# A mixture-of-experts kernel: four of eight experts, not three, on the 64-slot f32 path

## The chip, the cores and the metric

The kernel runs on one core of a Trainium2 chip. The metric is device time in microseconds of one launch, the median of three runs. Five engines work beside each other and meet at semaphores: TensorE (PE, matrix products), VectorE (DVE), ScalarE (ACT), GpSimd (POOL) and SyncE (SP), which here issues nearly all loads from the chip's main memory (HBM) into on-chip memory. The loads run on 16 DMA engines.

## What is computed

A trunk of two layers over 256 latent tokens of 1024 numbers. Layer 0 is attention and a dense SwiGLU; layer 1 is a gated convolution and a mixture of eight experts, of which each token takes two. The change lies in the mixture of experts:

```python
def swiglu(h, w_gate, w_up, w_down):
    return (jax.nn.silu(h @ w_gate) * (h @ w_up)) @ w_down

def moe_swiglu(h, router_w, w_gate, w_up, w_down):
    logits = (h @ router_w).astype(jnp.float32)
    top_vals, top_idx = lax.top_k(logits, TOP_K)
    weights = jax.nn.softmax(top_vals, axis=-1)
    gates = jnp.sum(jax.nn.one_hot(top_idx, N_EXPERTS) * weights[..., None], axis=-2)
    out = gates[..., 0:1] * swiglu(h, w_gate[0], w_up[0], w_down[0])
    for e in range(1, N_EXPERTS):
        out = out + gates[..., e:e + 1] * swiglu(h, w_gate[e], w_up[e], w_down[e])
    return out
```

All is f32. An expert has gate and up matrices of 1024 x 3584 and a down matrix of 3584 x 1024: 44 MB in all, 352 MB for the eight.

## The kernel before

**Ranks and slots.** The 256 tokens make 512 picks, so a list has 64 tokens on average. The kernel sorts experts by the length of their lists (function `ranks`): expert 0 always has rank 1, so that its weights can be loaded before the sort is known, and the others follow, longest first. The first `NE - NL` ranks are *heavy* and have 128 slots, the last `NL` are *light* and have `CAP` = 64. A list longer than its slots sets a flag, and a second pass over all eight experts (`spill`) does the rest; it is left out when the flag is 0.

**Chunks.** Each expert's 3584 hidden columns are done in seven chunks of 512 (`NFC`). A chunk takes six tiles of 1 MB from HBM: gate and up for the first half of the 1024 inputs, the same for the second half, and two of the down matrix. The down product of a chunk is computed while the next chunk is on, after its gate and up products.

**A heavy chunk** has f32 weights which ACT (line 75) and DVE (line 76) split into two parts `hi` and `lo`, in halves of a tile (`parts`), twelve splits for a chunk. PE then makes three products in the faster `fp32r` form (`mac`, lines 305, 307, 309): 48 of 128 x 512 for gate and up, 24 for down. The parts lie in a pool of five pairs, so splits run at most about five halves ahead of PE. A raw tile is free again when it is split.

**A light chunk** takes the raw tiles as they are. `pair` (line 1371) makes one f32 product for each of two halves of PE's columns, 64 slots each: gate in one half and up in the other, or two halves of the down matrix's columns. A light chunk has 16 such matmuls for gate and up and 8 for down, and the profile records each as two. A raw tile is free when PE has used it.

```python
def pair(ps, lhsT, ws, first, last):
    for m, w in enumerate(ws):
        pe.matmul(ps[m * CAP:(m + 1) * CAP], lhsT, w, start=first, stop=last, tile_position=(0, m * CAP))
```

**The order of chunks** comes from a list, written out below. The first four chunks are heavy, the last four light, and the rest are merged evenly by `sorted`. With H for heavy and L for light, the order before is HHHHH L HH L HH L H L HH L ... HH L H LLLL (35 H, 21 L).

```python
heavy = [(r, c) for r in range(NE - NL) for c in range(NFC)]
light = [(r, c) for r in range(NE - NL, NE) for c in range(NFC)]
mixed = [((2 * n + 1) / len(v), m, rc) for m, v in enumerate((heavy[4:], light[:-4])) for n, rc in enumerate(v)]
chunks = heavy[:4] + [rc for *_, rc in sorted(mixed)] + light[-4:]
```

**Loads.** SP issues the tiles in the order of the chunks into a ring of 13 tiles (`spare`, `load`, line 68). A load waits until the tile that stood in its place is free, and those behind it wait with it. When a new expert is due, two chunks ahead, POOL gathers its tokens' rows (`fetch_rows`, line 1284) into a tile of the same ring; PE transposes them (`turn_rows`, line 1298) one chunk ahead, and with that the tile is free. When an expert is done, its rows go back to the tokens by a product with the one-hot matrix (`output`, `scatter`, line 1391).

Of the kernel before, what the change touches and what calls it, by code (L numbers as in the profile page):

```python
# [20 lines left out]
FC = 512  # L21
NFC = 3584 // FC
NG = 2816 // 256
NL = 3
CAP = 64
EPS = 1e-6
FLAT = [*range(20, 24), *range(28, 40), 44, 45]
# [7 lines left out]
def trunk(ctx, tc, i, out, dbg=None):  # L35
# [52 lines left out]
# [4 lines that stand above are left out]
# [3 lines left out]
    def weights(m, r, c, h):  # L95
        def ap():
            if r and r not in who:
                who[r] = nc.values_load(cur["who"][0:1, r:r + 1], engines=[mybir.EngineType.SP], min_val=0, max_val=NE - 1)
            return i[m][who[r] if r else 0, c, h]
        return ap  # L100

    whole += [False] * len(order)
    for n in range(len(chunks) + 1):
        if n < len(chunks):
            order += [weights(m, *chunks[n], h) for h in range(2) for m in ("moe_g", "moe_u")]
            whole += [chunks[n][0] >= NE - NL] * 4
        if n:
            order += [weights("moe_d", *chunks[n - 1], h) for h in range(2)]
            whole += [chunks[n - 1][0] >= NE - NL] * 2
    LEAD = 7  # L110
# [1094 lines left out]
    def ranks():  # L1205
# [19 lines left out]
        cur["who"] = idx  # L1225
        dve.tensor_scalar(cap, rank, NE - NL + 0.5, CAP - 128.0, op0=OP.is_gt, op1=OP.mult)
        dve.tensor_scalar(cap, cap, 128.0, None, op0=OP.add)
# [182 lines left out]
    for r, E in enumerate(experts):  # L1410
        E.r, E.light = r, r >= NE - NL
        E.ys, E.eh, E.el = [None, None], [None, None], [None, None]
# [287 lines left out]
```

## Time and profile before

| what | value |
|---|---|
| median of three runs | 1395.54 us (1393.89 to 1396.03) |
| the profiled execution: its time / its span | 1395.5 us / 1393.6 us |
| PE busy | 1353.8 us, 97% |
| DVE busy, ACT busy | 964.0 us (69%), 796.5 us (57%) |
| bytes read from HBM | 470.22 MB, of them 352 MB for the experts |
| chain that ended last | PE 85%, DMA 6%, DVE 4%, ACT 3% |

The span is the time from the first to the last instruction; what lies between it and the run's time is outside the program. Matmuls overlap each other in PE's pipeline, so a mean duration of one matmul is longer than the time from one to the next, and a PE that shows 97% need not be at its peak. The mixture of experts takes from about 495 us to the end.

### The profile page before, as it was taken

To read this page: it belongs to the slowest core of one execution; us is meant where nothing else is said; L and a number is where in the kernel's file an instruction comes from. 1 tells how busy PE (TensorE), PEld (TensorE's weight loads), DVE (VectorE), ACT (ScalarE), POOL (GpSimd) and SP (SyncE) were. 2 spreads that over 40 slices of the span, in tenths; PEclk is the share of its full clock that TensorE was granted. 3 is DMA by queue.
4 is the path that set the end of the run, shared out by engine and by line. 5 is a ranking of instruction groups with operands and counts; after the bars stand their busy time and mean duration, and the time that the engine had idled before them with its cause. 6 is when DMAs were issued, how large, how long until landed. Compare 5 with 4: busy or idle time off the path is not lost.

```text
span 1393.6 us, 19980 instructions
## 1 busy us (share of the span) xinstructions
PE 1353.8 (97%) x7496; PEld 990.2 (71%) x7496; DVE 964.0 (69%) x1257; ACT 796.5 (57%) x1070; POOL 10.8 (1%) x13
## 2 busy tenths in 40 slices
PE   6988999999999999999999999999999999999997
PEld 4766789999889977766666766667667666676742
DVE  4777768677677688866767767767577677676721
ACT  5566765444464377756656666656567566565610
POOL 0000000000000000000000000000000000000000
PEclk9999999999999999999999999999999999999999
DMA  9733778678657399797999999998999999999994
GB/s 374 281 121 117 277 270 334 242 284 311 251 237 266 147 380 358 274 420 320 420 420 421 420 380 420 409 400 365 419 413 422 415 374 386 408 421 417 416 421 166
DMA packets 67161, 473.70 MB, mean 340 GB/s; under 512 B 7472, under 2 KB 8112, under 8 KB 11120
## 3 DMA queue, kind: packets, MB, share of 16 engines
q1 hardware_dynamic: 66240, 469.46, 84.2%
q0 software_dynamic: 816, 2.88, 0.6%
q8 instruction: 61, 1.00, 0.3%
q14 instruction: 44, 0.36, 0.1%
HBM read 470.22 MB, written 2.10 MB: 339 GB/s over the span
## 4 chain that ended last, share of the span: by engine, by line
PE 85%; DMA 6%; DVE 4%; ACT 3%; issue 1%; SPq 0%; ACTq 0%; DVEq 0%
PE pm L1371 10%; PE pm L305 8%; PE pm L307 8%; PE pm L309 8%; PE acc L305 8%; PE acc L307 7%; PE acc L309 7%; PE acc L1371 5%; DMA raw<-in_moe_g_dram 5%; PE pm L961 4%; PE pm L963 4%; PE pm L962 4%; PE pm L1351 2%; DMA raw<-in_moe_d_dram 1%; PE pm L186 1%; DVE lo L76 1%
## 5 line engine op out<-in xcount | busy, mean ns | idle before, releaser
L76 DVE TENSOR_TENSOR lo<-raw,hi 128x1024 fp32r<-128x1024 f32 x522 | 628.6, 1222 | 157.1 <-ACT hi L75 133.1
L75 ACT ACTIVATE hi<-raw 128x1024 fp32r<-128x1024 f32 x522 | 545.6, 1060 | 256.5 <-PE pm L309 107.7
L305 PE MATMUL pm<-hi,eh 128*128 128x512 f32 x560 | 226.2, 404 | 0.4 <-ACT g L291 0.2
L307 PE MATMUL pm<-lo,eh 128*128 128x512 f32 x560 | 220.2, 393 | 2.2 <-DVE lo L76 2.0
L309 PE MATMUL pm<-hi,el 128*128 128x512 f32 x560 | 219.5, 392 | 0.0
L1371 PE MATMUL pm<-raw,hl 128*64 128x512 f32 x672 | 155.4, 599 | 0.0
L963 PE MATMUL pm<-th,lo 128*128 128x256 f32 x480 | 135.9, 283 | 0.0
L962 PE MATMUL pm<-tl,hi 128*128 128x256 f32 x480 | 135.7, 283 | 0.0
L961 PE MATMUL pm<-th,hi 128*128 128x256 f32 x480 | 135.6, 283 | 0.0
L305 PEld LDWEIGHTS pm<-hi,eh 128*128 128x128 f32 x560 | 105.8, 189 | 33.9 <-issue 8.1
L307 PEld LDWEIGHTS pm<-lo,eh 128*128 128x128 f32 x560 | 106.0, 189 | 24.5 <-DVE lo L76 4.6
L309 PEld LDWEIGHTS pm<-hi,el 128*128 128x128 f32 x560 | 105.7, 189 | 22.9
L1371 PEld LDWEIGHTS pm<-raw,hl 128*64 128x64 f32 x672 | 44.1, 136 | 80.5 <-issue 77.6
L961 PEld LDWEIGHTS pm<-th,hi 128*128 128x128 f32 x480 | 91.2, 190 | 0.8 <-issue 0.4
L962 PEld LDWEIGHTS pm<-tl,hi 128*128 128x128 f32 x480 | 91.0, 189 | 0.4
L963 PEld LDWEIGHTS pm<-th,lo 128*128 128x128 f32 x480 | 91.1, 190 | 0.0
L305 PE MATMUL acc<-hi,dh 128*128 128x512 f32 x280 | 88.7, 398 | 0.0
L307 PE MATMUL acc<-lo,dh 128*128 128x512 f32 x280 | 86.5, 390 | 0.0
L309 PE MATMUL acc<-hi,dl 128*128 128x512 f32 x280 | 86.3, 389 | 0.0
L1365 DVE TENSOR_TENSOR sg<-pm,sg 128x512 f32<-128x512 f32 (+1 forms) x56 | 38.5, 688 | 64.5 <-ACT sg L1364 64.2
L1371 PE MATMUL acc<-raw,dT 128*64 128x512 f32 x336 | 78.1, 600 | 0.0
L1364 ACT ACTIVATE sg<-pm 128x512 f32<-128x512 f32 (+1 forms) x56 | 32.7, 584 | 69.5 <-PE pm L1371 66.4
(331 smaller groups left out, 1568.0 us busy)
## 6 DMA issues: line engine op xcount, KB each, us to landing
raw<-in_moe_d_dram SPq DMA_DIRECT2D x112, 1024.0 KB, 12.8
raw<-in_moe_g_dram SPq DMA_DIRECT2D x111, 1024.0 KB, 12.9
raw<-in_moe_u_dram SPq DMA_DIRECT2D x111, 1024.0 KB, 12.8
raw<-in_ada_w_dram SPq DMA_DIRECT2D x48, 1024.0 KB, 6.2
raw<-in_conv_i_dram SPq DMA_DIRECT2D x12, 1024.0 KB, 7.0
raw<-in_ffn_g_dram SPq DMA_DIRECT2D x11, 1024.0 KB, 6.9
raw<-in_ffn_u_dram SPq DMA_DIRECT2D x11, 1024.0 KB, 4.8
raw<-in_ffn_d_dram SPq DMA_DIRECT2D x11, 1024.0 KB, 4.9
```

Source lines behind the costliest of these rows:

```text
L75: act.activation(hi, r, AF.Copy)
L76: dve.tensor_sub(lo, r, hi.bitcast(F32))
L305: pe.matmul(p, hh, wh[j], start=first, stop=False)
L307: pe.matmul(p, hh, wl[j], start=False, stop=False)
L309: pe.matmul(p, hl, wh[j], start=False, stop=last)
L961: pe.matmul(d, hi[:, c], th[:, k], start=(k == 0), stop=False)
L962: pe.matmul(d, hi[:, c], tl[:, k], start=False, stop=False)
L963: pe.matmul(d, lo[:, c], th[:, k], start=False, stop=(k == KD - 1))
L1351: pe.transpose(C.ps[:, k * w:(k + 1) * w], C.hd[:, k * 128:(k + 1) * 128], ident[0:w, 0:w])
L1364: act.activation(sg, C.g, AF.Silu)
L1365: dve.tensor_mul(sg, C.u, sg)
L1371: pe.matmul(ps[m * CAP:(m + 1) * CAP], lhsT, w, start=first, stop=last, tile_position=(0, m * CAP))
```

## The change

One constant: the four lowest ranks are light, not three.

```diff
 NFC = 3584 // FC
 NG = 2816 // 256
-NL = 3
+NL = 4
 CAP = 64
```

`NL` decides which ranks are heavy, which loads are taken whole (without a split), the slots of each rank, and by the list above the order of chunks. There are now 28 H and 28 L: HHHHH L H L H L ... H L LLLL, where H and L alternate from the fifth chunk on, and the last four are L as before.

On PE, the first place that differs is behind the down product of chunk 5, the first light one (`acc<-raw,dT`). `pm<-hi,eh` is a heavy gate or up product, `pm<-raw,hl` a light one, `cid,sg` the transposes of the chunk before. Before:

```order
L307 MATMUL pm<-lo,eh_5292 128x512
L309 MATMUL pm<-hi,el_5293 128x512
L1371 MATMUL acc<-raw,dT 64x512 x8
L305 MATMUL pm<-hi,eh_5270 128x512
L307 MATMUL pm<-lo,eh_5270 128x512
```

And now:

```order
L1371 MATMUL acc<-raw,dT 64x512 x8
L1371 MATMUL pm<-raw,hl 64x512 x6
L1351 MATMUL pm<-cid,sg 128x128 x4
L1371 MATMUL pm<-raw,hl 64x512 x10
L305 MATMUL acc<-hi,dh 128x512 x2
L307 MATMUL acc<-lo,dh 128x512 x2
L309 MATMUL acc<-hi,dl 128x512 x2
```

Chunk 7 was heavy, with 48 products for gate and up; it is light, with 16. The down product of chunk 6 follows it.

On SP, the same place in the queue of loads. A load that has an `ISA` row ahead of it takes its address from the expert number that SP reads from the sort, so it belongs to a rank above 1:

```order
 L68 DMA raw<-in_moe_d_dram 128x2048
-L68 DMA raw<-in_moe_g_dram 128x2048
-L68 DMA raw<-in_moe_u_dram 128x2048
-L68 DMA raw<-in_moe_g_dram 128x2048
-L68 DMA raw<-in_moe_u_dram 128x2048
-L68 DMA raw<-in_moe_d_dram 128x2048 x2
+L68 ISA
+L68 DMA raw<-in_moe_g_dram 128x2048
+L68 ISA
+L68 DMA raw<-in_moe_u_dram 128x2048
```

The tiles are as many as before (SP has 1005 rows in both), and gate, up and down follow each other as before. What moves is whose tiles they are: from here every second chunk's tiles are a light expert's.

## Rows read from the trace of the kernel before

**Rows 1.** The page: PE's share, then DMA share and GB/s in 40 slices.
```profile
PE 1353.8 (97%) x7496; PEld 990.2 (71%) x7496; DVE 964.0 (69%) x1257; ACT 796.5 (57%) x1070; POOL 10.8 (1%) x13
...
DMA  9733778678657399797999999998999999999994
GB/s 374 281 121 117 277 270 334 242 284 311 251 237 266 147 380 358 274 420 320 420 420 421 420 380 420 409 400 365 419 413 422 415 374 386 408 421 417 416 421 166
```

**Rows 2.** Stretches: busy time of each engine, granted clock, DMA share, GB/s.
```profile
579.00:1371.50 792.50, 786.71 (x3528) 513.47 (x3530) 541.49 (x534) 462.80 (x539) 8.27 (x6) 1.00 0.98 404
1371.50:1393.60 22.10, 13.49 (x64) 4.36 (x60) 3.92 (x6) 1.08 (x3) 0.00 (x0) 0.92 0.15 52
653.50:805.00 151.50, 149.38 (x672) 101.26 (x672) 108.59 (x104) 92.28 (x102) 1.76 (x1) 1.00 1.01 420
...
898.50:901.80 3.30, 3.30 (x9) 2.54 (x9) 3.27 (x5) 0.80 (x2) 0.00 (x0) 0.50 0.99 407
```

**Rows 3.** The chain that ended last, in order of time: start, us, what.
```profile
653.56 20.82 DMA raw<-in_moe_g_dram
...
1126.79 1.87 PE pm L1371 x8
...
1174.14 1.87 PE pm L1371 x8
...
1206.99 2.58 PE pm L1371 x12
...
1255.81 2.73 PE pm L1371 x12
...
1301.35 2.73 PE pm L1371 x12
...
1329.85 2.58 PE pm L1371 x12
...
1343.13 2.73 PE pm L1371 x12
...
1355.73 2.58 PE pm L1371 x12
...
1378.56 4.47 PE acc L1371 x20
1383.05 0.76 DVE raw L1529
```

**Rows 4.** Groups by line: count, busy and mean of one, idle before.
```profile
L76 DVE TENSOR_TENSOR lo<-raw,hi 128x1024 fp32r<-128x1024 f32 x522 | 628.6, 1222 | 157.1 <-ACT hi L75 133.1 <-issue 1.2
...
L305 PE MATMUL pm<-hi,eh 128*128 128x512 f32 x560 | 226.2, 404 | 0.4 <-ACT g L291 0.2
...
L1371 PE MATMUL pm<-raw,hl 128*64 128x512 f32 x672 | 155.4, 599 | 0.0
```

**Rows 5.** Timeline of SP's issues of loads: start, us.
```profile
564.76 2.61 SPq L68 DMA_DIRECT2D raw<-in_moe_d_dram  x2
578.98 0.33 SPq L68 DMA_DIRECT2D raw<-in_moe_g_dram  x1
...
624.55 0.33 SPq L68 DMA_DIRECT2D raw<-in_moe_u_dram  x1
643.41 0.91 SPq L68 DMA_DIRECT2D raw<-in_moe_d_dram  x2
644.56 0.33 SPq L68 DMA_DIRECT2D raw<-in_moe_g_dram  x1
```

**Rows 6.** What SP's queue waited for: us in total, times, longest.
```profile
SPq L68 <- PE pm L1371: 186.8, 36, 18.4
...
SPq L68 <- PE pm L1298: 58.3, 5, 15.8
```

**Rows 7.** Timeline of PE at 895.79: start, us, what, idle before.
```profile
895.79 0.39 PE L309 MATMUL pm<-hi,el 128*128 128x512 f32 x1
897.92 0.46 PE L1391 MATMUL pm<-yh,ohTl 64*128 64x512 f32 x1 [1.74 <-DVE dl L1360]
```

## The prediction, made before the changed kernel ran

> **What bounds the kernel now.** I read the page first. TensorE (PE) is busy 97% of the span, and the slices of DMA show 9 nearly everywhere after the middle, at about 420 GB/s [rows 1]. Both could be the bound, so the next view is the table of stretches. From 579.0 us, where loads start again after a pause [rows 5], to 1371.5 us, where the last has landed, the core moved 404 GB/s at a share of 0.98; in the stretch 653.5 to 805.0 it moved 420 at 1.01 [rows 2], and the best long slices show 421 [rows 1]. So 421 GB/s is all that the loads get here, and one tile of 1,048,576 bytes takes 1.049 / 0.421 = 2.49 us. A chunk of an expert is six such tiles (two halves each of gate, up and down): 14.95 us of DMA, whoever computes it.
>
> The chain that ended last gives PE's side. It runs through PE almost without a break, and the first PE piece of each 64-slot chunk stands in it [rows 3]. I call a 128-slot chunk H and a 64-slot chunk L. From 1255.81 to 1301.35 lie one L and two H without a change of expert: 45.54 us. From 1301.35 to 1329.85 lie one L and one H: 28.50 us. Hence H = 45.54 - 28.50 = 17.04 us and L = 28.50 - 17.04 = 11.46 us of PE. Two L in a row, 1343.13 to 1355.73, took 12.60, with products of the heavy expert's output in it. DMA wants 3 x 14.95 = 44.9 us for the first pattern, PE 45.54. **The kernel before is PE-bound by 1 to 2%, with DMA close behind.** This is the reading on which all else rests.
>
> **The change, part by part.** The list says which chunks become L: the rank-5 expert's seven.
>
> *Does it still fit?* The lists are not in the trace, but they follow from the reference's inputs (seed 0): counting the two largest logits of each token gives 77, 51, 73, 39, 56, 48, 101, 67 for experts 0 to 7. Expert 0 is forced to rank 1; the others sort to 101, 73, 67 | 56, 51, 48, 39. The newly light expert has 56 slots, so 64 hold it and the spill pass is not entered. Its cost otherwise is below.
>
> *PE.* Removed: 7 H, that is 7 x 72 three-product matmuls and some wide transposes. Added: 7 L, that is 7 x 24 f32 matmuls, each shown as two records. One H to one L is 17.04 - 11.46 = 5.58 us, times 7 = **39.1 us**. The groups agree on the kind of saving: 560 of each three-product line for gate and up against 672 records of the pair line [rows 4]; these means overlap, so the periods of the chain are the price, not the means. Bounds: if every new L cost what L after L costs (12.60), 7 x 4.44 = 31.1; there are still only the four L at the end in such a row, plus one, so I take 39.1.
>
> *DVE and ACT.* 7 x 12 splits go from each. On DVE a split takes 1.222 us [rows 4], so 103 us of work vanish, but DVE's waits lie behind PE and the chain holds little of it: **0** on the path. PE and DMA cover it; without that cover it could only help.
>
> *Gather and output.* One gather of 128 rows becomes 64, one output step of two becomes one, and which chunk each stands in moves. Per change of expert the chain shows 1126.79 to 1174.14 = 47.35 against 45.54 (1.8 more) and 1174.14 to 1206.99 = 32.85 against 28.50 (4.35 more) [rows 3]. There are seven changes of expert before and seven after. I take **0**, within 3 us either way.
>
> *DMA.* No load is removed. Only the order of H and L changes, from mostly H H L to H L H L, and the first PE difference is chunk 7, so the program up to 579 us stays. From there DMA has 404 x 792.5 = 320.2 MB to move, and what follows 1371.5, 52 x 22.1 = 1.1 MB, is the output alone [rows 2]; at 421 GB/s without a pause that is 760.5 us, so the last load lands at 579.0 + 760.5 = 1339.5 at the earliest, 32 us earlier than now. Behind it must come the last two down products and the end. In the row at 1378.56 five steps of a light down product take 4.47 us, so two take 1.8; from 1383.05 to the end of the span is 10.55 [rows 3]. The floor of DMA is 1339.5 + 1.8 + 10.6 = **1351.9**.
>
> *PE's path* ends at 1393.6 - 39.1 = **1354.5**. The two bounds are under three microseconds apart: after the change an H L pair takes 28.5 us of PE and 29.9 of DMA, so between changes of expert DMA is the slower one, and the seven changes (1.8 to 4.4 us each, some 20 in all) give PE's path back what the 23 pairs let it gain (23 x 1.4 = 32). The difference of 12 us comes out of the lead that loads have over PE. The lead at the end is now 1383.0 - 1371.5 = 11.5 us, 9.7 of them more than the 1.8 that it must be; and chunk 51, so far H, becomes L, which uses up 5.6 more. So PE waits for loads near the end: 12 + 5.6 - 9.7 = 8 us at most, 0 if a full ring had held the lead down anyway. I take the middle, **4**.
>
> Here the skill has a figure. The Trainium skill, DMA: Bandwidth & Descriptors, section Bandwidth, puts the ceiling of the fabric at 435 GB/s, but says that transfers between HBM and SBUF are bound at about 358 GB/s per core. By 358 the 320.2 MB would need 894 us, and loads would bind so hard that no saving on PE is worth anything; but the kernel before moved them in 792.5, so it does not hold on this core, and gets no chance of its own. By 435 the floor of DMA would be 1327.5 us and PE alone would bind, at 1354.5.
>
> **The sum.** 1354.5 + 4 = 1358.5 us of span. The profiled execution took 1395.5 for a span of 1393.6, and the median of the runs is 1395.54, so 1.9 is added: **1360 us**, a gain of 35 us or 2.5%.
>
> **The rivals.**
>
> *A. The forecast:* PE's saving is paid out until loads bind. 1352 to 1370 us. For it: the pair of 28.50 us, which is exactly the new pattern, was measured while DMA was saturated. Against it: it is measured once without a change of expert.
>
> *B. The ring's pauses stay.* SP issues loads in order into 13 tiles, and a gather takes a tile of the same ring. After 624.55 SP issued nothing until 643.41, then a burst [rows 5]; SP's waits name the gather's transposes (58.3 us in 5 waits) and the L products (186.8 in 36) [rows 6]. Such pauses make up the 32 us between 404 and 421 GB/s. Now they fall where PE is the bound, and cost nothing. With half the chunks L, raw tiles are held by PE more often, and if the pauses stay whole, the last load lands at 1371.5 again and the end is 1371.5 + 12.4 + 1.9 = 1386; half of them, 1370. Against it: a pause needs a full ring, and a ring is full only when loads are ahead of PE, which the change makes rarer. 1370 to 1390 us.
>
> *C. Nothing comes of it:* more PE waits eat the last of B's gain too. 1393 to 1398 us. The clock would be the way. In the stretch 898.5 to 901.8 the granted clock is 0.50, that is 1.2 of 2.4 GHz, right after PE had waited 1.74 us at 897.92 for DVE [rows 2, 7]; nine matmuls there start 0.43 us apart rather than 0.23, so one such drop costs about 1.7 us beside its wait. If each of the 24 pairs ended in a wait of that size, 24 x (1.7 + 1.7) = 82 would eat all; one drop in four pairs adds 20. The stretch 653.5 to 805.0 shows the clock at 1.00 although the chain runs through a load for 20.82 us in it [rows 2, 3], which speaks against it. The Trainium skill, TensorE: Matmul & The Clock Gate, Part 1, has the array's clock fall after it has been less busy; the trace agrees as far as its drop stands behind a wait.
>
> *D. Slower:* the ring itself. An L holds its tiles until PE has used them, an H until DVE has split them. The stop behind 624.55 lies in the slice 627.1 to 662.0, at 319 GB/s: 34.8 x (1 - 319 / 421) = 8.4 us of DMA lost [rows 1]. If one like it came with the L of each of the 24 pairs, loads would need 24 x 8.4 = 202 us over their floor, and the end would be 1351.9 + 202 + 1.9, about 1556. The point that decides is (1393.6 - 1351.9) / 24 = 1.7 us of lost DMA per pair, where the gain is gone. The four L at the end run from 1329.85 on at the full 421 GB/s [rows 1, 3], which speaks against it. The spill pass would be worse (eight experts x 7 x 6 tiles x 2.49 = 837 us on top), but needs a fifth list of over 64, and it has 56.
>
> **How the numbers follow.** A has 0.70, B 0.21, C 0.04, D 0.05. A measurement of this kernel can tell about 0.2% (3 us) from no change. Faster by more than that: A and B and a little of C, 0.92; same 0.03; slower 0.05. The point is A's, 1360. The low end is the DMA floor less the small unknowns of the ends, 1351.9 + 1.9 - 2 = 1352. The high end takes in most of B: 1384. What lies above is the last of B, C and D, under 0.2 with what lies below.
>
> **What would show it.** PE's H L pairs at 28.5 to 30 us in the chain; splits on DVE down by 84; GB/s from 579 on at 415 to 421, with the last load landing at 1340 to 1350 us; the ring's long stops on SP fewer; waits of PE for moe loads near the end, a few us in all. B would show as GB/s still at 404 and holes in the issues of loads. C would show as more stretches at a clock of 0.5. The forecast is wrong altogether if the pattern H L costs PE more than 28.5 us, or if the flag for the spill is set.

## The result: 31.6 us faster, and where they came from

The changed kernel takes **1364.18 us** (median of 4 runs, 1361.22 to 1366.28) against 1395.78 of the kernel before: a ratio of 0.9774, with a 95% interval from 0.9754 to 0.9795. The forecast was 1360. The profiled execution took 1361.22 us for a span of 1359.4; the forecast for the span was 1358.5.

The page of the changed kernel, with the rows that answer to [rows 1], and the shares of the chain that ended last:

```profile
PE 1310.8 (96%) x7328; PEld 916.1 (67%) x7328; DVE 858.4 (63%) x1164; ACT 700.8 (52%) x975; POOL 8.2 (1%) x13
...
DMA  9833769678749469699999999999999999999996
GB/s 378 293 124 101 276 268 351 244 279 310 279 171 338 174 269 385 255 422 420 420 421 420 409 421 421 404 420 420 421 404 421 407 422 419 420 408 421 421 419 254
...
PE 78%; DMA 9%; DVE 6%; ACT 4%; issue 2%; SPq 0%; ACTq 0%; DVEq 0%
```

PE has 43.0 us less to do (1353.8 before, 1310.8 now). The slices of GB/s from the eighteenth to the last but one show 404 to 422; before, they went down to 320, 365 and 374. The stretches, as in [rows 2]: from where the loads start again to where the last has landed, what follows it, and one stretch with the same bounds as in the experiments below.

```profile
575.80:1345.90 770.10, 755.90 (x3404) 444.02 (x3406) 436.63 (x442) 368.46 (x446) 5.57 (x6) 1.00 1.01 415
1345.90:1359.40 13.50, 4.55 (x20) 1.26 (x16) 3.23 (x5) 0.00 (x0) 0.00 (x0) 0.84 0.24 83
...
579.00:1345.00 766.00, 751.80 (x3387) 441.07 (x3387) 433.47 (x438) 366.72 (x444) 5.57 (x6) 1.00 1.01 416
```

The loads run at 415 GB/s where they had 404, and the last lands at 1345.9 us, 25.6 us earlier. PE is busy 98.1% of the last stretch: 751.80 of 766.00. The clock is 1.00. So neither the 421 GB/s that a free stretch shows nor an unbroken PE is reached, and both are missed by 1 to 2%.

The Trainium skill, HBM Reference, Specifications (TRN2), says that a core which streams alone measures about 425 GB/s, while its share with both cores of a pair at work is about 358. The 415 to 421 GB/s of this one-core kernel agree with the first figure.

The chain of the changed kernel in order of time, as in [rows 3]: two pieces that begin a light chunk, a load, the piece of PE behind it, and the last light down product.

```profile
957.35 19.68 DMA raw<-in_moe_g_dram
981.29 1.01 PE pm L1371 x4
...
1256.12 2.58 PE pm L1371 x12
1284.47 2.58 PE pm L1371 x12
...
1344.02 4.47 PE acc L1371 x20
```

A pair H L without a change of expert takes 1284.47 - 1256.12 = 28.35 us of PE; the forecast said 28.50. The load of 19.68 us that the chain runs through at 957.35 is one that PE came to wait for, by a way that the waits show. The groups, as in [rows 4]:

```profile
L76 DVE TENSOR_TENSOR lo<-raw,hi 128x1024 fp32r<-128x1024 f32 x438 | 524.8, 1223 | 180.5 <-ACT hi L75 163.0 <-issue 1.2
...
L1371 PE MATMUL pm<-raw,hl 128*64 128x512 f32 x896 | 207.5, 600 | 3.5 <-DVE xhat L1398 3.2 <-PE acc L1371 0.3
L305 PE MATMUL pm<-hi,eh 128*128 128x512 f32 x448 | 179.0, 400 | 0.2 <-ACT g L291 0.2
```

The counts are those of the change: 522 - 438 = 84 splits fewer, 224 light records more, 112 matmuls fewer in each three-product line of gate and up. The mean of one kind is as before.

What is new is the list of waits (engine, what it waited for, us in total, times, longest). The three rows of SP's queue are of the whole span, and the lower two answer to [rows 6]; the others are of 579 to 1345 us.

```profile
SPq L68 <- PE acc L1371: 177.9, 47, 10.0
SPq L68 <- PE pm L1371: 167.2, 49, 8.2
...
SPq L68 <- PE pm L1298: 44.9, 6, 11.5
...
ACT hi L75 <- DMA raw<-in_moe_d_dram: 75.2, 39, 5.6
...
PE pm L1336 <- DVE oh L1276: 6.2, 3, 2.4
...
PE pm L1371 <- DVE xhat L1398: 3.2, 3, 1.1
...
PE pm L1351 <- DVE sg L1365: 2.8, 3, 1.2
```

SP stops more often for light products, and on average for a shorter time: 96 stops of 345.1 us together, gate, up and down, where the kernel before had 69 of 292.6, that is 3.6 us each for 4.2. The longest for gate and up fell from 18.4 to 8.2 us; the longest for a down product rose from 7.3 to 10.0. ACT, which makes the first half of a split, now waits 39 times for a down tile, 75.2 us in all; in the kernel before it was 4 times and 10.4 us over the whole span. And PE waits for DVE at three places, 12.2 us in these rows; in the same stretch of the kernel before no line of PE waited for more than 1.7 us.

One of these waits of the changed kernel can be followed through the three engines from 968 to 984 us (start, us busy, what, idle before it and its releaser). DVE:

```profile
973.10 4.86 DVE L76 TENSOR_TENSOR lo<-raw,hi 128x1024 fp32r<-128x1024 f32 x4 [5.39 <-ACT hi L75]
978.23 1.23 DVE L76 TENSOR_TENSOR lo<-raw,hi 128x1024 fp32r<-128x1024 f32 x1 [0.27 <-ACT hi L75]
979.49 0.69 DVE L1365 TENSOR_TENSOR sg<-pm,sg 128x512 f32<-128x512 f32 x1
980.10 0.47 DVE L1276 TENSOR_SCALAR oh<-cst,posr 128x128 f32<-128x128 f32 x2
```

ACT in the same time:

```profile
972.01 2.00 ACT L75 ACTIVATE hi<-raw 128x1024 fp32r<-128x1024 f32 x2 [5.29 <-DMA raw<-in_moe_d_dram]
...
977.14 1.06 ACT L75 ACTIVATE hi<-raw 128x1024 fp32r<-128x1024 f32 x1 [0.62 <-DMA raw<-in_moe_g_dram]
```

And PE:

```profile
980.52 0.43 PE L1336 MATMUL pm<-cid,oh 128*128 128x128 f32 x2 [2.45 <-DVE oh L1276]
```

PE needs `oh`, a mask of 0.47 us that says which tokens are the next expert's. It depends on no load. But it stands on DVE's queue behind five splits. The first four of these waited 5.39 us for ACT, and ACT had waited 5.29 us for a down tile; the fifth waited 0.27 us more, for the gate tile that the chain above shows landing at 957.35 + 19.68 = 977.03. So late loads stop PE through work that has nothing to do with them. The Trainium skill, PSUM — Partial Sum Buffer, Engine vs sequencer instructions, calls the queues of these engines strictly first in, first out; these rows agree.

### The profile page after: what moved, and what is told of

It reads as the page before. It is cut to its first block, busy times and chain, and to the rows that moved or that the text cites. A ratio compares the mean times of both kernels' runs of the same rounds, so it can differ in the third digit from the quotient of the medians.

```text
span 1359.4 us, 19330 instructions
## 1 busy us (share of the span) xinstructions
PE 1310.8 (96%) x7328; PEld 916.1 (67%) x7328; DVE 858.4 (63%) x1164; ACT 700.8 (52%) x975; POOL 8.2 (1%) x13
## 4 chain that ended last, share of the span: by engine, by line
PE 78%; DMA 9%; DVE 6%; ACT 4%; issue 2%; SPq 0%; ACTq 0%; DVEq 0%
PE pm L1371 14%; DMA raw<-in_moe_g_dram 7%; PE acc L305 6%; PE acc L307 6%; PE acc L309 6%; PE pm L305 5%; PE pm L307 5%; PE pm L309 5%; PE acc L1371 5%; PE pm L961 4%; PE pm L963 4%; PE pm L962 4%; DVE lo L76 3%; DMA raw<-in_moe_d_dram 2%; PE pm L1351 2%
## 5 line engine op out<-in xcount | busy, mean ns | idle before, releaser
L76 DVE TENSOR_TENSOR lo<-raw,hi 128x1024 fp32r<-128x1024 f32 x438 | 524.8, 1223 | 180.5 <-ACT hi L75 163.0
L75 ACT ACTIVATE hi<-raw 128x1024 fp32r<-128x1024 f32 x438 | 452.8, 1058 | 251.7 <-DMA raw<-in_moe_d_dram 75.5
L1371 PE MATMUL pm<-raw,hl 128*64 128x512 f32 x896 | 207.5, 600 | 3.5 <-DVE xhat L1398 3.2
L305 PE MATMUL pm<-hi,eh 128*128 128x512 f32 x448 | 179.0, 400 | 0.2 <-ACT g L291 0.2
L307 PE MATMUL pm<-lo,eh 128*128 128x512 f32 x448 | 175.5, 392 | 2.1 <-DVE lo L76 2.0
L309 PE MATMUL pm<-hi,el 128*128 128x512 f32 x448 | 174.6, 390 | 0.0
L1371 PE MATMUL acc<-raw,dT 128*64 128x512 f32 x448 | 103.9, 599 | 0.0
L307 PEld LDWEIGHTS pm<-lo,eh 128*128 128x128 f32 x448 | 84.2, 188 | 20.5 <-DVE lo L76 4.5
L305 PEld LDWEIGHTS pm<-hi,eh 128*128 128x128 f32 x448 | 84.1, 188 | 19.8 <-issue 0.7
L309 PEld LDWEIGHTS pm<-hi,el 128*128 128x128 f32 x448 | 84.1, 188 | 17.8
L1364 ACT ACTIVATE sg<-pm 128x512 f32<-128x512 f32 (+1 forms) x56 | 32.8, 586 | 99.4 <-PE pm L1371 97.1
## 6 DMA issues: line engine op xcount, KB each, us to landing
raw<-in_moe_u_dram SPq DMA_DIRECT2D x111, 1024.0 KB, 14.3
```

Source lines behind the costliest of these rows:

```text
L75: act.activation(hi, r, AF.Copy)
L76: dve.tensor_sub(lo, r, hi.bitcast(F32))
L305: pe.matmul(p, hh, wh[j], start=first, stop=False)
L307: pe.matmul(p, hh, wl[j], start=False, stop=False)
L309: pe.matmul(p, hl, wh[j], start=False, stop=last)
L1364: act.activation(sg, C.g, AF.Silu)
```

## The experiments

The names: H is a chunk of 128 slots, L one of 64. Ratios are to the kernel before on the same chip, with the 95% interval. Lines of code that are added move later line numbers: by 2 in the two kernels with half down tiles and the two with blocks of four, by 4 in the first and by 3 in the second of those with doubled splits. In code cuts, `...` stands for lines left out.

### Are the loads a bound? Half of each light down tile, in both kernels

In both kernels the light experts' down tiles are loaded by half, and that half is used in place of both: half of the light down weights are left out, and PE does the same work.

```diff
+            downs.update((len(order) - 2, len(order) - 1))
...
-                    at[1] = load(src)
+                    n = 1024 if whole[u] and u in downs else 2048
+                    at[1] = load(src[:, :n], n)
...
-            f = [slice(s % 2 * 1024 + 512 * q, s % 2 * 1024 + 512 * q + 512) for q in range(2)]
+            f = [slice(512 * q, 512 * q + 512) for q in range(2)]
```

In the changed kernel:

> The changed kernel with the down tiles of all light chunks loaded by half (1024 of 2048 columns) and the half used twice, so part of the down product is replaced by another part; the matmuls are as many and of the same sizes. Loads lose 28 x 2 x 0.524 = 29.4 MB, 70 us at 421 GB/s. If loads bind the changed kernel: the time falls to PE's own path, forecast at 1354.5 us of span, so 1350 to 1358 us. If PE binds it already: 1362 to 1366 us, no change.

It took 1353.71 us, ratio 0.9696 (0.9677 to 0.9714), with a span of 1351.9. Its stretch from 579 us on:

```profile
579.00:1323.50 744.50, 739.68 (x3342) 438.83 (x3342) 439.02 (x442) 371.93 (x443) 6.61 (x6) 1.00 0.97 390
```

Its waits from 579 to 1345 us, two lines:

```profile
ACT hi L75 <- DMA raw<-in_moe_d_dram: 3.5, 5, 1.6
...
PE pm L1373 <- DVE xhat L1400: 3.2, 3, 1.1
```

With less to load (390 GB/s are enough, at a DMA share of 0.97), PE is busy 99.4% of the stretch, ACT's wait for down tiles falls from 75.2 to 3.5 us, and of PE's three waits those for `oh` and `sg` are gone; the one for `xhat` (L1373 and L1400 here) stays. What the loads still cost the changed kernel is 1359.4 - 1351.9 = 7.5 us by the spans, and (0.9774 - 0.9696) x 1395 = 10.9 us by the ratios. The ratios are the fairer of the two: the profiled execution of the changed kernel was the fastest of its four.

In the kernel before:

> The same halved down tiles of light chunks in the kernel before (three light ranks), again with one half used twice: 22.0 MB less, 52 us at 421 GB/s. If PE bound the kernel before (my theory): at most the 6 us of waits for loads around 650 us, so 1388 to 1396 us, and its distance to the same edit of the changed kernel is PE's 39 us. If loads bound it too: down by most of 52 us, to about 1350.

1392.59 us, ratio 0.9989 (0.9977 to 1.0001), span 1390.3.

```profile
579.00:1371.00 792.00, 787.68 (x3542) 512.65 (x3542) 540.15 (x533) 462.69 (x538) 7.22 (x6) 1.00 0.93 376
```

At 376 GB/s with PE busy 99.5% the time hardly moves: the kernel before was bound by PE. The spans of the two differ by 1390.3 - 1351.9 = 38.4 us, and the ratios by 0.0293, or 40.9 us. PE is busy over 99% in both here, so this is the change's price on PE's path.

### Do the splits matter? Two ways to put them back

The 84 splits that the change removes are put back as second, idle halves of other splits of H tiles: each of 84 does its ACT copy and its DVE subtraction twice, with the same result. First in the order copy, subtract, copy, subtract:

```diff
-            ready[at[0]] = parts(at[1][:, h * 1024:(h + 1) * 1024], cur[p])
+            r = at[1][:, h * 1024:(h + 1) * 1024]
+            hi, lo = ready[at[0]] = parts(r, cur[p])
+            if u >= FIRST and u % 2 and h:
+                act.activation(hi, r, AF.Copy)
+                dve.tensor_sub(lo, r, hi.bitcast(F32))
```

> The changed kernel with 84 of its heavy splits made twice on ACT and DVE, so that these engines do as many splits as before the change (103 us of DVE, 89 of ACT); results are the same. If the splits that the change removes were worth nothing on the path (my step): 1362 to 1368 us. If relief of DVE and ACT carried the gain: 1375 to 1395 us.

1415.76 us, ratio 1.0175 (1.015 to 1.02): slower than the kernel before, and outside both ranges. Its waits from 579 us on begin to say why:

```profile
ACT hi L136 <- DVE lo L76: 128.7, 74, 3.5
```

The second copy writes `hi` again, so it must wait until the first subtraction has read it. That wait is the experiment's own, and the run says nothing on the splits. In the next kernel both copies come ahead of both subtractions:

```diff
-        act.activation(hi, r, AF.Copy)
-        dve.tensor_sub(lo, r, hi.bitcast(F32))
+        for _ in range(2 if twice else 1):
+            act.activation(hi, r, AF.Copy)
+        for _ in range(2 if twice else 1):
+            dve.tensor_sub(lo, r, hi.bitcast(F32))
...
+            ready[at[0]] = parts(r, cur[p], u >= FIRST and u % 2 and h)
```

> Again 84 heavy splits made twice, but now as two ACT copies in a row and then two DVE subtractions in a row, so that no engine waits for the other between them; the run before had ACT wait 129 us for DVE in its second copies, which is a wait of my making and no work. Results are the same. If the splits that the change removed were worth nothing on the path: 1362 to 1370 us. If 103 us of DVE work in the heavy chunks cannot be hidden: 1385 to 1415 us.

1383.7 us, ratio 0.9918 (0.9906 to 0.9931): some 20 us slower than the changed kernel, between the two ranges and 1.3 us short of the second. The profiled execution was the slowest of six, 1388.25 us, that is 27.0 us more than that of the changed kernel; the rows below are to be weighed against these 27.0. SP's issues of loads, first in the changed kernel (start, us, what), to be held against 578.98 in [rows 5]:

```profile
561.65 2.61 SPq L68 DMA_DIRECT2D raw<-in_moe_d_dram  x2
575.85 0.33 SPq L68 DMA_DIRECT2D raw<-in_moe_g_dram  x1
```

then with the doubled splits:

```profile
575.51 2.56 SPq L68 DMA_DIRECT2D raw<-in_moe_d_dram  x2
...
588.61 0.33 SPq L68 DMA_DIRECT2D raw<-in_moe_g_dram  x1
```

12.8 us are lost before the loads have started again: 15 of the doubled splits (15 x 1.22 = 18 us of DVE) lie in the first five H, which stand in a row. The other 69, 84 us of DVE work, go with the remaining 14.3. An estimate from rows: an H has 12 splits of 1.22 us on DVE and two products of 0.69 (`sg` and `dl`), 16.0 us of PE's 17.04. Three more splits make 19.7, which is 2.7 us over, or 13 us for five H; 12.8 were measured. So where H follows H, DVE has little room, and splits are not free to add. Where H and L alternate and the sum leaves room, PE waited 9.7 us for `lo` and 2.2 for `hi` in gate and up products from 579 to 1345 us; in the changed kernel it was 1.6 for `lo`. It doesn't follow that taking splits away paid: the pair of runs above comes out within 2 us of PE's share as forecast.

### One more light expert

The fifth-longest list has 67 tokens, so this kernel drops three of them; the second pass for longer lists is kept from being taken. That is the part of the computation that it leaves out.

```diff
-NL = 4
+NL = 5
...
-    mixed = [((2 * n + 1) / len(v), m, rc) for m, v in enumerate((heavy[4:], light[:-4])) for n, rc in enumerate(v)]
-    chunks = heavy[:4] + [rc for *_, rc in sorted(mixed)] + light[-4:]
+    mixed = [((2 * n + 1) / len(v), m, rc) for m, v in enumerate((heavy[5:], light[:-4])) for n, rc in enumerate(v)]
+    chunks = heavy[:5] + [rc for *_, rc in sorted(mixed)] + light[-4:]
...
-        dve.tensor_scalar(over, most, 0.5, None, op0=OP.is_gt)
+        dve.tensor_scalar(over, most, 1.5, None, op0=OP.is_gt)
```

> Five light ranks in place of four, the mixture of H and L starting at chunk 5 as in the changed kernel. The fifth list has 67 tokens, and the flag for the second pass is kept at 0, so what lies beyond 64 slots of that list is left out of the result. PE loses another 7 x 5.58 = 39.1 us, loads lose nothing. If loads bind the changed kernel (my theory): 1355 to 1366 us, at most the 9 us that loads still stand idle behind 580 us. If PE's path still binds it: about 1364 - 39 = 1325 us.

1376.17 us, ratio 0.986 (0.9842 to 0.9878): 12 us slower than with four, and neither theory had that. Its stretch from 579 us to the last load:

```profile
579.00:1361.00 782.00, 731.67 (x3248) 375.27 (x3247) 328.49 (x351) 273.67 (x352) 5.51 (x6) 0.98 0.99 408
```

On its page, the shares of the chain that ended last:

```profile
PE 65%; DMA 21%; DVE 8%; ACT 4%; issue 2%; SPq 0%; ACTq 0%; DVEq 0%
```

And two of its waits in the stretch:

```profile
ACT hi L75 <- DMA raw<-in_moe_g_dram: 154.2, 28, 13.0
...
PE pm L1351 <- DVE sg L1365: 27.7, 14, 3.3
```

PE is busy 20 us less than the changed kernel in its shorter stretch, the chain lies in DMA for 21%, and still the loads are slower, 408 GB/s. A kernel that is bound by loads alone should run them at 421, or at least at the 415 of the changed kernel. ACT stands for 13.0 us at a time before a gate tile, and PE waits 14 times for `sg`, the product that DVE makes from ACT's Silu. This asks for the order of the chunks, which the next two kernels test with four light experts.

### The order alone: blocks of four

All counts stay. H and L come in blocks of four rather than in turn (the last block of H has three).

```diff
-    chunks = heavy[:4] + [rc for *_, rc in sorted(mixed)] + light[-4:]
+    chunks = heavy[:5]
+    for n in range(7):
+        chunks += light[4 * n:4 * n + 4] + heavy[5 + 4 * n:9 + 4 * n]
```

> The changed kernel with the same 28 H and 28 L, but in blocks: five H, then four L and four H in turn, four L at the end. The sums of PE and of loads are the same. If only the sums count and the ring evens out a block (a block of four H lets loads gain 8 us on PE, one of four L lets PE gain 10 to 14): 1362 to 1370 us. If the even alternation is part of the gain: over 1375 us, with GB/s behind 580 us well under 416.

1398.77 us, ratio 1.0025 (1.0013 to 1.0036): the whole gain is gone, with the same products, splits and loads. The stretch of the comparison, and a short one behind a wait:

```profile
579.00:1345.00 766.00, 721.65 (x3221) 435.15 (x3220) 423.65 (x431) 363.27 (x436) 7.42 (x6) 0.96 0.98 402
...
1271.00:1276.00 5.00, 4.44 (x14) 1.74 (x16) 4.60 (x5) 2.08 (x3) 0.00 (x0) 0.50 1.02 421
```

Its waits from 579 us on:

```profile
PE pm L1353 <- DVE sg L1367: 35.1, 5, 9.2
```

ACT at the end of one block of L, where the splits for the next H begin (L1366 is the Silu):

```profile
1267.33 2.00 ACT L75 ACTIVATE hi<-raw 128x1024 fp32r<-128x1024 f32 x2 [14.69 <-DMA raw<-in_moe_g_dram]
1269.24 0.57 ACT L1366 ACTIVATE sg<-pm 64x512 f32<-64x512 f32 x1
```

and PE there:

```profile
1260.25 2.75 PE L1373 MATMUL pm<-raw,hl 128*64 128x512 f32 x12
1271.56 0.69 PE L1353 MATMUL pm<-cid,sg 64*128 64x64 f32 x4 [8.56 <-DVE sg L1367]
```

PE has finished the light products by 1263.0. The Silu on them takes 0.57 us, but ACT's queue has two splits of a gate tile ahead of it, and the tile lands late. ACT stands for 14.69 us, the Silu comes at 1269.24, DVE's product `sg` stands behind the second parts of the same two splits, and PE goes on at 1271.56, with the granted clock at 0.50, that is 1.2 of 2.4 GHz, in the stretch behind the wait. The splits ahead are there because a chunk's work looks up to nine tiles ahead for something to split.

### The same blocks, with a nearer look-ahead

The last kernel with one edit more: a light chunk looks ahead by six tiles, not nine, so that the Silu stands before the splits of the next H on ACT, and `sg` before them on DVE.

```diff
-        while split and k <= most[0] and k // 2 - n // 2 < 9:
+        while split and k <= most[0] and k // 2 - n // 2 < (6 if step == 2 else 9):
```

> The blocks of four again, but a light chunk looks only 6 tiles ahead for splits in place of 9, so that on ACT the Silu of the last L of a block stands ahead of the first splits of the next H, and not behind them. In the run with blocks PE waited 35 us in the transposes (line 1351) for DVE's product, which waited for that Silu, which stood behind splits that waited for loads. If that order on ACT carries the loss of the blocks: 25 to 38 us less than the 1399 of that run, 1361 to 1374. If the ring and the sums of a block carry it: 1394 to 1402.

1363.57 us, ratio 0.9793 (0.9767 to 0.9818): all is back. The stretch:

```profile
579.00:1345.00 766.00, 747.41 (x3382) 443.30 (x3382) 429.50 (x441) 365.74 (x444) 6.89 (x6) 0.99 1.01 416
```

ACT at the end of such a block of L:

```profile
1229.74 0.59 ACT L1366 ACTIVATE sg<-pm 64x512 f32<-64x512 f32 x1 [3.61 <-PE pm L1373]
1241.27 2.00 ACT L75 ACTIVATE hi<-raw 128x1024 fp32r<-128x1024 f32 x2 [10.94 <-DMA raw<-in_moe_g_dram]
```

ACT still waits 10.94 us for a gate tile, but the Silu is done before, and PE doesn't notice. So the 35 us of the blocks came from the order of splits and short results on the queues of ACT and DVE, not from the blocks as such. The edit can also move a gather's place in the ring of tiles, but SP's stops behind gathers (its waits for line 1300 from 579 to 1345 us) are nearly the same, 23.2 us with the blocks and 21.4 with the nearer look-ahead. For the kernel with five light experts, which showed the same wait for `sg`, this cause is argued and wasn't tried.

### Can the last 7 to 11 us be had?

Five kernels tried. First, the light experts' turn begins one chunk earlier, so that DMA has work where it moved 340 GB/s, from 495 to 579 us; the one-hot matrix of expert 0 and its transposes, which sat at chunk 2, go to chunk 6.

```diff
-    mixed = [((2 * n + 1) / len(v), m, rc) for m, v in enumerate((heavy[4:], light[:-4])) for n, rc in enumerate(v)]
+    mixed = [((2 * n + 1) / len(v), m, rc) for m, v in enumerate((light[:-4], heavy[4:])) for n, rc in enumerate(v)]
...
-            hook(2, 1, choice, E, pos)
+            hook(6, 1, choice, E, pos)
...
```

> The changed kernel with the merge turned round, so that L H L H starts with L at chunk 4 in place of 5; expert 0's one-hot matrix and its transposes move from chunk 2 to chunk 6. Loads are idle some 15 us between 539 and 581 us, where five H in a row are PE-bound. If loads bind all that follows, an L one chunk earlier gives back up to 5.6 us of this: 1357 to 1361 us. If not: 1362 to 1366.

1364.02 us, ratio 0.9771 (0.9752 to 0.9789): no different from the changed kernel. Its stretches:

```profile
495.00:579.00 84.00, 83.46 (x398) 64.81 (x398) 70.26 (x103) 64.44 (x76) 4.03 (x1) 0.99 0.95 377
579.00:1342.80 763.80, 748.13 (x3362) 442.48 (x3362) 437.08 (x441) 369.62 (x447) 5.55 (x6) 1.00 1.00 414
1342.80:1360.90 18.10, 9.39 (x44) 2.94 (x40) 3.93 (x6) 0.96 (x2) 0.00 (x0) 0.91 0.17 62
```

The loads did come forward, to 377 GB/s from 495 to 579 us (340 in the changed kernel), and the last landed at 1342.8, 3.1 us earlier. But the tail behind it grew from 13.5 to 18.1 us, with 44 matmul records in it for 20: now PE was late. Its waits from 579 to 1345 us had not shrunk: 6.1 us for `oh`, 4.1 for `sg`, 3.9 for `xhat` and 1.6 for `lo`, 15.7 us for 13.8 in the changed kernel, and ACT's for down tiles were 76.0 us for 75.2.

Second, the same with two L rather than four at the very end (`light[:-2]` and `light[-2:]` in these lines):

> As the run with L at chunk 4, and with two L at the end in place of four, the other two spread through the mixture. If loads bind to the end, where the L stand makes no difference: as that run, within 3 us. If PE's lead near the end matters (loads must be ahead of four L in a row): 4 to 8 us less than that run.

1365.25 us, ratio 0.9785 (0.9768 to 0.9803): no difference.

Third, the changed kernel with the step that makes `oh` earlier on DVE, for every expert but the first light one (the first step of the fourth chunk ahead, where it was step 10 of the third):

```diff
-            hook(n - 3, 10, choice, E, posr)
+            hook(*((n - 3, 10) if r == NE - NL else (n - 4, 1)), choice, E, posr)
```

> The changed kernel with DVE's one-hot matrix for the next expert (line 1276) made almost a chunk earlier for every expert but the first light one. In the changed kernel PE waits 6.2 us for it in three places (the transposes at line 1336), because in DVE's order it stands behind splits that wait for a load. If these waits are part of what lies between PE's own path (1351.9 us of span with the halved loads) and 1359.4: 1358 to 1362 us, 2 to 5 less than the 1364 of the changed kernel. If the loads' end sets the time whatever PE waits for: 1363 to 1366.

1361.87 us, ratio 0.9769 (0.9748 to 0.9789): not to be told from the changed kernel. Its waits from 579 us on:

```profile
ACT hi L75 <- DMA raw<-in_moe_d_dram: 85.7, 39, 7.1
...
PE pm L1371 <- issue: 5.2, 3, 1.9
```

PE no longer waits for `oh`, which cost 6.2 us, and the time stays. In its place PE waits 5.2 us at three others, each before the first product of a new light expert. The trace names no releaser there ("issue"), but DVE's rows do. One of the three, DVE first, then PE:

```profile
1007.19 2.36 DVE L76 TENSOR_TENSOR lo<-raw,hi 128x1024 fp32r<-128x1024 f32 x2 [6.87 <-ACT hi L75]
...
1010.30 0.69 DVE L1304 TENSOR_TENSOR hl<-hl,ada 128x512 f32<-128x512 f32 x1
...
1011.10 2.80 PE L1371 MATMUL pm<-raw,hl 128*64 128x512 f32 x12 [1.69 <-issue]
```

`hl` holds the new expert's tokens, and PE starts 0.1 us after DVE has finished it (1010.99); the other two (797.02 and 1225.11) go the same way. `hl` stands on DVE behind two splits of a down tile that ACT had waited for (6.97 us in that place, 85.7 in all where it was 75.2). So the wait has moved some 30 us on, about two chunks, behind the same kind of late tile, and PE's lines over 1 us sum to 15.1 us for 13.8. Fourth, both together:

> L from chunk 4 on and the one-hot matrix early, both. With L from chunk 4 on the last load landed 3 us earlier, yet the run was no faster: its end was PE's. If the one gives loads 3 us and the other PE 6 us: 1356 to 1360 us. If either still binds alone: 1362 to 1366.

1362.17 us, ratio 0.9778 (0.976 to 0.9796). PE's lines over 1 us sum to 16.1 us, the `oh` line gone and others longer. And with the nearer look-ahead as well:

> As the run with L from chunk 4 on and the one-hot matrix early, and with the look-ahead of 6 tiles in light chunks. In an even alternation the first splits of the next H then stand behind the Silu of the L or H before. If ACT's order costs the alternation anything: 1 to 4 us less than that run. If the splits come too late for PE then: up to 10 us more.

1363.07 us, ratio 0.9785 (0.9767 to 0.9802). So the nearer look-ahead gives nothing by itself, and what it gave back above was the loss of the blocks. None of the five beats the changed kernel by what a measurement can tell. In the first and the fourth the range for a gain was missed by 2 to 3 us, and the range for none holds the time; the second is within 3 us of the first, as one of its ranges said; the third lies just inside its range for a gain, 2.3 us under the changed kernel, which is within noise; the fifth is 0.9 us over the fourth, which is noise as well.

## Why the prediction was right, step by step

**PE bound the kernel before: shown.** When it needed only 376 GB/s for 404, it went 0.1% faster, within what a measurement can tell.

**39.1 us off PE's path: right.** The two kernels that are free of their loads differ by 38.4 us of span, or 40.9 by the ratios. The pair H L took 28.35 us for 28.50. PE's path, forecast to end at 1354.5, ended at 1351.9 in the kernel with half down tiles, mostly because the kernel before, by the same edit, ends 3.3 us sooner too (1390.3 for 1393.6).

**Loads bind next: right, though not by the floor.** The floor put the last landing at 1339.5 us at the earliest, and the span at 1351.9. The landing was at 1345.9, 6.4 us later. The loads began 3.1 us sooner (575.85 for 578.98), with no edit ahead of them, and lost 11 us on the way: 770.1 us at 415 GB/s are 319.6 MB, for which 421 need 759.1 (the remaining 1.4 us is the rounding of these figures in MB). The tail was 13.5 us for 12.4. But a floor at the end is not how the loads bind: with the last landing 3.1 us sooner the time stayed, and with fewer late tiles on the way it fell by 10.9 us.

**"PE waits for loads near the end, 0 to 8, taken 4": the term that was mis-sized.** It measured 7.5 us by the spans and 10.9 by the ratios. That the sum, 1358.5 us, lies within 1 us of the profiled span is luck: PE's path was forecast 2.6 us too long and this wait 3.5 too short. Its place was wrong too. PE waits around changes of expert along the way, not at the end, and not for the tiles of its own light products: where the loads are the cause (`oh` and `sg`, gone with half down tiles), it waits for short results of DVE that stand behind splits whose tile is late. The working took PE's lead over the loads as one number; in the kernel it is each engine's queue that must have a lead. The list of PE's waits bears the size out: the four lines over 1 us of the changed kernel from 579 to 1345 us sum to 13.8 us (6.2, 3.2, 2.8 and 1.6 for a split), the two of the kernel with half down tiles to 4.8 (3.2 and 1.6).

**Splits removed, 0: right as used.** No gain beyond PE's share shows: 38.4 and 40.9 us against 39.1. But the reason given, that PE and DMA cover them, holds in one direction alone: put back (as second copies of other splits), they cost 20 us.

**Gather and output, 0 within 3:** no run takes this apart from the rest.

**Rival B** (the ring's pauses stay) came true by about a third: the loads lost 11 us to 421 GB/s where they had lost 32. **Rival C** had the right mechanism, a wait of PE and the clock behind it, but the changed kernel is too seldom in it: the clock is 1.00 from 579 to 1345 us. The blocks of four show what it does when the waits are long: 0.96, and no gain. **Rival D** (the ring held by light tiles) wasn't seen: blocks of four hold it most, and with the order on ACT mended they ran at 416 GB/s.

What stays open is why loads that start earlier do not shorten PE's waits (the first of the last five kernels). The list of waits says that PE's end was late there because the same waits at changes of expert stood, 15.7 us in all; no run says why the 3 us that loads had gained did not reach these places.

## What to carry to other kernels

When a saving brings two bounds within 1% of each other, price the order of the work as carefully as its amount: here the order alone was worth the whole gain. On an engine that works in order, look for long work fetched ahead that waits for a load and stands before a short result that the bound engine needs; the list of waits names the short result, and only the timeline of the engine in between shows what it stood behind. Removing one wait that the list names can pay nothing: as long as the loads came no sooner, PE stood as long about two chunks further on.

## What the runs showed of the hardware that was not expected

A wait of PE can cost more than its length, and its length alone doesn't say when. Behind the 8.56 us at 1271.56 in the blocks of four, the granted clock was 0.50 from 1271 to 1276 us. Behind 2.45 us at 980.52 in the changed kernel it stayed at 1.00 (from 980.5 to 984 us), though behind 1.74 us in the kernel before (and one of 0.72 us some 4 us ahead of that) it had been 0.50 [rows 2, 7]. What else decides was not tried. Over 579 to 1345 us the clock was 0.96 with the blocks of four and 1.00 in the changed kernel.

Less work on PE need not make loads faster, because PE also frees their tiles. With five light experts PE had less to do, but it stood 27.7 us for `sg`; SP's stops for its gate and up products of L (line 1371, from 579 to 1345 us) came to 261.2 us where the changed kernel had 167.2, and the rate was 408 GB/s where it ran at 415 to 416. That the stops come from PE's waits is argued, not tried.
